# The last output group of a conformer layer in three token spans (256, 128, 128) instead of two halves

## The chip, the cores and the metric

One core of a Trainium2 chip runs the whole program. The metric is the device time of one execution in microseconds (us). The engines are named as in the profile: PE (TensorE matmuls), PEld (TensorE weight loads, which overlap PE), DVE (VectorE), ACT (ScalarE), POOL (GpSimd) and SP (SyncE, which issues the DMAs).

## What is computed

The reference at DEPTH = 1, with 512 tokens and a model width of 2048, is one conformer convolution module, one squared-ReLU MLP and a final norm, all in float32:

```python
h = x + conformer_conv(rms_norm(x, norm_mix_g), ...)
h = h + square(relu(rms_norm(h, norm_ffn_g) @ w_up)) @ w_down     # w_down: 8192 x 2048
return rms_norm(h, final_norm_g)       # y * rsqrt(mean(y*y, -1) + 1e-5) * g
```

## The kernel before

Activations lie transposed: 128 partitions hold 128 of the 2048 channels, and the free dimension holds the 512 tokens. The residual stream is `hT[0..3]`, four tiles of 4 x 512 columns. Each product of float32 operands is split in two float32r parts, and `mm3` makes it of three matmuls (hi x hi, hi x lo, lo x hi, L209 to L211), each with its own load of 128 x 128 weights.

The MLP's 8192 hidden channels come in units of 256. Every few units, a "down" job multiplies them by `w_down` and adds the result to `hT`. Its four output groups (512 output channels each) go through `group`: four PSUM banks, one for each 128 output channels `m`; pieces `p` of 256 rows of weights; and for each piece two blocks of rows `kk`, four `m` and three matmuls, so 24 matmuls for a piece. The last down job has four units, thus four pieces in a group (p = 0 to 3), 96 matmuls.

The last group of the last job is split by tokens. With `split` = 4 all four pieces run for the tokens 0 to 255 and then all four for 256 to 511, so 96 matmuls of 256 columns for each half; the loop over `m` is then outside that over `kk`. PE's order is the program's order. `hooks` are called ahead of the matmuls of a given (first token, piece, m) and put other work there. For the halves they are:

- (256, p 0, m 0): `finish(0)`: for each m, DVE adds the bank to `hT[3]` (L995), ACT squares it (L996), DVE adds the square to Q3 (L998, L1000); then ACT multiplies by the norm's gain (L1003).
- (256, 0, 3): `fin_sum`: column sums of Q3 over the partitions, as plain float32 matmuls of one moving column with Q3 as the weights (L243); then DVE (`ms_fin`, L255), POOL (the power -1/2, L257) and DVE (`dg_fin`, L222) make a diagonal of the norm's scales.
- (256, 1, 2): `fin_scale`: one plain float32 matmul (L232) spreads the scales to all partitions. Nine multiplications (`fin_parts`: two of one 128-channel row of blocks, seven of two) scale `hT`; two of them are on POOL. Nine stores on SP's queue follow (L1034).
- (256, 3, 0): `fin_head`: the column sums of Q3 for the second half, which holds only groups 0 to 2; the squares of group 3 are added at the end, with four more parts.

After the last matmul of the group stand `finish(256)`, `fin_sum(256)` and `fin_scale(256)`, with all nine multiplications on DVE. In blocks under `manual_schedule(engines=ordered)` the work of DVE, ACT and POOL stays in the order written.

Of the kernel before, what the change touches and what calls it, by code (L numbers as in the profile page):

```python
# [8 lines left out]
F32 = mybir.dt.float32  # L9
# [5 lines left out]
P = 128  # L15
T = 512
# [11 lines left out]
HT = T // 2  # L28
# [18 lines left out]
LN_FIRST = (3, 6)  # L47
UNIT = 256
N_UNITS = DFF // UNIT
FIN_POOL = (4, 8), ()  # L50


@with_exitstack
def conformer_layer(ctx: ExitStack, tc: tile.TileContext, xT, vecs, wdw, w1, w2, wupb, wdn, outT):
    nc = tc.nc
# [3 lines left out]
    wpool = ctx.enter_context(tc.tile_pool(name="wpool", bufs=WBUFS))  # L59
# [26 lines left out]
    def col(base, k):  # L86
        return vec[:, base + k : base + k + 1]
# [109 lines left out]
    def prep(upto):  # L197
        fetch(upto + 2)
        while state["prep"] < min(upto, len(pieces)):
            i = state["prep"]  # L200
            state["prep"] += 1
            if pieces[i][1] is BLOCKS:
                split_blocks(i)
                continue
            split_hi(i)
            split_lo(i, nc.gpsimd if FIRST_POOL <= i < n_p1 else nc.vector)
# [8 lines left out]
    def bank(tag, name):  # L215
        return pp.tile([P, T], F32, tag=tag, name=name, bufs=banks_of[tag])

    def diag(r, name, pool):
        n = r.shape[1]
        tag, bufs = ("diag", 2) if pool is ph1 else ("z", 3)  # L220
        dg = pool.tile([P, 4, P], F32, tag=tag, name=f"dg_{name}", bufs=bufs)[:, 0:n]
        nc.vector.tensor_tensor(  # L222
            out=dg,
            in0=ident[:, None, :].to_broadcast([P, n, P]),
            in1=r[:, :, None].to_broadcast([P, n, P]),
            op=ALU.mult,
        )
        return dg

    def spread(dg, out, start=True):  # L230

        nc.tensor.matmul(  # L232
            out, lhsT=ones, rhs=dg.rearrange("p a b -> p (a b)"), start=start, stop=True, skip_group_check=True
        )
        return out

    def colsum(b, c0, parts, t0, n, first, last, neg=0):

        for i, part in enumerate(parts):
            for t in range(n):
                nc.tensor.matmul(  # L243
                    b[:, c0 + t : c0 + t + 1],
                    lhsT=part[:, t0 + t * P : t0 + (t + 1) * P],
                    rhs=invd[:, neg : neg + 1],
                    start=first and i == 0 and t == 0,
                    stop=last and i == len(parts) - 1,
                    skip_group_check=True,
                )  # L250

    def rms_scale(b, name, pool, n=4):

        ms = pool.tile([P, n], F32, tag=f"ms{n}", name=f"ms_{name}", bufs=2)
        nc.vector.tensor_scalar_add(out=ms, in0=b[:, 0:n], scalar1=EPS)  # L255
        r = pool.tile([P, n], F32, tag=f"rr{n}", name=f"rr_{name}", bufs=2)
        nc.gpsimd.tensor_tensor(out=r, in0=ms, in1=mhalf[:, 0:n], op=ALU.pow)  # L257
        return diag(r, name, pool)


    p1 = ExitStack()
# [63 lines left out]
    ordered = {mybir.EngineType.DVE, mybir.EngineType.Activation, mybir.EngineType.Pool}  # L325
    with tc.manual_schedule(engines=ordered):
        for k in range(NK):
            ah[k], al[k] = split_scaled(k, x_of(k), col(C_GMIX, k))
            i, kk = divmod(k, 2)
            if i < 2 or kk == 0:  # L330
# [4 lines left out]
                    out=lo[:, :, part], in0=r, in1=hi[:, :, part].bitcast(F32), op=ALU.subtract  # L335
# [44 lines left out]
    box = {}  # L380
# [376 lines left out]
    ng = {"n": 0}  # L757
    pi = {"i": n_p1}

    def group(nk, rows_hi, rows_lo, hooks=None, split=0):  # L760


        n = ng["n"]
        ng["n"] += 1
        banks = box["banks"] = [bank("mm" if n % 2 == 0 else "xxxy"[m], f"g{n}_{m}") for m in range(4)]
        i0 = pi["i"]
        pi["i"] += nk // 2
        spans = [(h * HT, HT, p) for h in range(2) for p in range(split)]
        spans += [(0, T, p) for p in range(split, nk // 2)]
        for t0, w, p in spans:  # L770
            prep(i0 + p + 3 if t0 or w == T else min(i0 + p + 3, i0 + split))
            wh, wl = prepped[i0 + p]
            tok = slice(t0, t0 + w)
            order = [(kk, m) for kk in range(2) for m in range(4)]
            if w < T:
                order = [(kk, m) for m in range(4) for kk in range(2)]
            for kk, m in order:
                if hooks and kk == 0 and (t0, p, m) in hooks:
                    hooks[t0, p, m]()
                k = 2 * p + kk  # L780
                c = slice(m * P, (m + 1) * P)
                mm3(
                    banks[m][:, tok],
                    wh[:, kk, c],
                    wl[:, kk, c],
                    rows_hi[k][:, tok],
                    rows_lo[k][:, tok],
                    k == 0 and t0 == 0,
                    k == nk - 1,
                    skip_group_check=split > 0,  # L790
                )
        return banks
# [34 lines left out]
    for g in range(4):  # L827
        hooks = {}
        if g == 0:
            hooks = dict(zip(LN_AT, (second_taps, second_sums, second_scale)))  # L830
        if g == 3:

            hooks = {(0, 2 + 2 * i, 0): (lambda kt: lambda: place(kt, blocks_of[kt]))(3 + i) for i in range(3)}
        banks = group(NK, sh, sl, hooks, split=4 if g == 0 else 0)
        if g == 0:
            ph2 = ctx.enter_context(tc.tile_pool(name="ph2", bufs=2, reuse_waits="tile"))
# [5 lines left out]
        for m in range(4):  # L842
            k = 4 * g + m
            h = hT[g][:, m, :]
            nc.vector.scalar_tensor_tensor(
                out=h, in0=banks[m], scalar=col(C_BPW2, k), in1=h, op0=ALU.add, op1=ALU.add
            )
            if m % 2 == 0:
# [3 lines left out]
                out=blocks[:, at : at + 2].rearrange("p a b -> p (a b)"), in_=h, func=AF.Copy, scale=col(C_GFFN, k)  # L852
# [100 lines left out]
    Q3 = None  # L953
    for kind, what in jobs[:-1]:
# [4 lines left out]
        for g in range(4):  # L959
            banks = group(2 * len(what), zh, zl)  # L960
            for m in range(4):
                h = hT[g][:, m, :]
# [4 lines left out]
    Q3 = ph2.tile([P, T], F32, tag="Q2", name="Q3", bufs=1)  # L967
    sqo = [ph2.tile([P, 7, T], F32, tag=f"T{i}", name=f"sqo{i}", bufs=1) for i in range(3)]

    def sq_of(k):  # L970
        return sqo[k // 7][:, k % 7, :]

    for g in range(3):
        banks = group(kc, zh, zl)
        for m in range(4):
            k = 4 * g + m
            h = hT[g][:, m, :]
# [8 lines left out]


    sqs = [sq_of(12 + m) for m in range(4)]

    def finish(t0):  # L990
        tok = slice(t0, t0 + HT)
        with tc.manual_schedule(engines=ordered):
            for m in range(4):
                h = hT[3][:, m, tok]
                nc.vector.tensor_add(out=h, in0=h, in1=box["banks"][m][:, tok])  # L995
                nc.scalar.activation(out=sqs[m][:, tok], in_=h, func=AF.Square)  # L996
                if t0 == 0 and m:
                    nc.vector.tensor_add(out=Q3[:, tok], in0=Q3[:, tok], in1=sqs[m - 1][:, tok])  # L998
            if t0 == 0:
                nc.vector.tensor_add(out=Q3[:, tok], in0=Q3[:, tok], in1=sqs[3][:, tok])  # L1000
            for m in range(4):
                h = hT[3][:, m, tok]
                nc.scalar.activation(out=h, in_=h, func=AF.Copy, scale=col(C_GFIN, 12 + m))  # L1003

    def fin_sum(t0=0):
        if t0 == 0:
            b = bank("mm", "cs_fin0")
            colsum(b, 0, [Q3], t0, 2, True, True)
        else:
            b = box["csb"]  # L1010
            colsum(b, 0, sqs, t0, 2, False, True)
        with tc.manual_schedule(engines=ordered):
            box["dg"] = rms_scale(b, f"fin{t0}", ph2, 2)

    def fin_head():
        box["csb"] = bank("mm", "cs_finb")
        colsum(box["csb"], 0, [Q3], HT, 2, True, False)

    def fin_scale(t0=0):
        tok = slice(t0, t0 + HT)  # L1020
        rf = spread(box["dg"], bank("mm", f"sp_fin{t0}")[:, 0:HT])
        rfs = ph2.tile([P, T], F32, tag="W", name=f"rfs{t0}", bufs=1)[:, 0:HT]
        with tc.manual_schedule(engines=ordered):
            if FIN_POOL[t0 > 0]:
                nc.scalar.copy(out=rfs, in_=rf)
            for i, (g, m, n) in enumerate(fin_parts):
                h2 = hT[g][:, m : m + n, tok]
                if i in FIN_POOL[t0 > 0]:
                    nc.gpsimd.tensor_mul(out=h2, in0=h2, in1=rfs[:, None, :].to_broadcast([P, n, HT]))
                else:  # L1030
                    nc.vector.tensor_mul(out=h2, in0=h2, in1=rf[:, None, :].to_broadcast([P, n, HT]))
        for g, m, n in fin_parts:
            k = 4 * g + m
            nc.sync.dma_start(  # L1034
                out=outT[k * P : (k + n) * P, tok].rearrange("(k p) t -> p k t", p=P),
                in_=hT[g][:, m : m + n, tok],
            )

    fin_parts = [(0, 0, 1), (0, 1, 1)] + [(i // 2, i % 2 * 2, 2) for i in range(1, 8)]

    group(
        kc,
        zh,
        zl,
        {(HT, 0, 0): lambda: finish(0), (HT, 0, 3): fin_sum, (HT, 1, 2): fin_scale, (HT, 3, 0): fin_head},
        split=kc // 2,
    )
    finish(HT)
    fin_sum(HT)
    fin_scale(HT)  # L1050


# [48 lines left out]
```

## Time and profile before

| | us |
|---|---|
| median of 3 runs | 1927.95 (1926.95 to 1928.57) |
| profiled execution, its own time | 1929.58 |
| its span, first to last instruction | 1927.5 |
| PE busy | 1905.0 (99% of the span) |
| DVE / ACT / POOL busy | 1377.4 / 742.4 / 349.4 |
| first matmul of the last group | 1889.90 from the span's start |
| first matmul of its second half | 1901.41 |
| last matmul of the group | 1914.11 |

PE is busy nearly throughout. Only the last 13 us, after the last matmul of the group, belong to the other engines and the stores. A timeline row gives the start, the length, the engine, the line and the operation with its output and input; matmuls overlap in time, so that the distance between two starts, not the length, is what one costs in a stream.

### The profile page before, as it was taken

Reading aid. Unit: us, or ns where it says so; the run is one execution under the profiler, and the core shown is the slowest. Engines: PE = TensorE matmul, PEld = TensorE weight load, DVE = VectorE, ACT = ScalarE, POOL = GpSimd, SP = SyncE. Lnnn points to the kernel's source line nnn. Section 1 sums busy time; section 2 is a strip of 40 time slices with the busy share of each in tenths; the row PEclk is TensorE's granted clock in tenths of the full one; section 3 lists DMA queues with packets and bytes.
Section 4 is the critical chain, followed back from the end, with each engine's and each line's share of the span. In section 5 each row is a group of like instructions: output and inputs, shape, how many; then the busy total and the mean of one; then the engine's idle time right before and its main releaser. Section 6 shows DMA issues by size and latency. Waiting matters only on the chain.

```text
span 1927.5 us, 27676 instructions
## 1 busy us (share of the span) xinstructions
PE 1905.0 (99%) x11200; PEld 1699.8 (88%) x11200; DVE 1377.4 (71%) x1910; ACT 742.4 (39%) x910; POOL 349.4 (18%) x240
## 2 busy tenths in 40 slices
PE   9999999999999999999999999999999999999997
PEld 8888888888889898998989899898989989898987
DVE  6899998975568676776667677676767767676845
ACT  6544444554344242323324232332423324242433
POOL 1788998741211000000000000000000000000000
PEclk9999999999999999999999999999999999999999
DMA  7333333142323333323233332333333233233332
GB/s 247 88 99 98 99 89 109 46 147 93 98 83 104 99 110 89 117 90 111 88 99 116 93 110 88 110 94 102 112 88 110 88 120 92 96 110 91 118 98 99
DMA packets 134559, 199.24 MB, mean 103 GB/s; under 512 B 7200, under 2 KB 72992, under 8 KB 134432
## 3 DMA queue, kind: packets, MB, share of 16 engines
q1 hardware_dynamic: 134288, 197.41, 33.5%
q8 instruction: 87, 1.43, 0.3%
q14 instruction: 40, 0.33, 0.1%
q10 hardware_dynamic: 144, 0.07, 0.0%
HBM read 193.27 MB, written 4.19 MB: 102 GB/s over the span
## 4 chain that ended last, share of the span: by engine, by line
issue 68%; PE 26%; DVE 3%; POOL 1%; ACT 1%; DMA 0%; POOLq 0%; SPq 0%; DVEq 0%; ACTq 0%
PE g L210 3%; PE g L209 3%; PE g L211 3%; PE pa L210 2%; PE pg L211 2%; PE pg L210 2%; PE pa L211 2%; PE pg L209 2%; PE pa L209 2%; DVE acc L434 1%; PE pa L372 1%; PE pg L372 1%; DMA wr<-w 0%; POOL Q L859 0%; PE u L211 0%
## 5 line engine op out<-in xcount | busy, mean ns | idle before, releaser
L171 ACT CAST wh<-wr 128x1024 fp32r<-128x1024 f32 x215 | 225.7, 1050 | 500.1 <-PE g L210 321.1
L209 PE MATMUL g<-z,wh 128*128 128x512 f32 (+1 forms) x1016 | 391.1, 385 | 0.0
L210 PE MATMUL g<-z,wh 128*128 128x512 f32 (+1 forms) x1016 | 390.8, 385 | 0.0
L211 PE MATMUL g<-z,wl 128*128 128x512 f32 (+1 forms) x1016 | 390.7, 385 | 0.0
L176 DVE TENSOR_TENSOR wl<-wr,wh 128x1024 fp32r<-128x1024 f32 x158 | 201.1, 1273 | 207.8 <-ACT wh L171 207.7
L211 PE MATMUL u<-slot,wl 128*128 128x256 f32 x1120 | 317.8, 284 | 1.6 <-DVE wl L195 1.0
L209 PE MATMUL u<-slot,wh 128*128 128x256 f32 x1120 | 318.0, 284 | 0.0
L210 PE MATMUL u<-slot,wh 128*128 128x256 f32 x1120 | 317.5, 283 | 0.0
L195 DVE TENSOR_TENSOR wl<-ws,wh 128x1024 fp32r<-128x1024 f32 x128 | 156.7, 1224 | 160.2 <-ACT wh L194 160.2
L434 DVE SCALAR_TENSOR_TENSOR acc<-u,wd,acc 128x512 f32<-128x512 f32 (+1 forms) x360 | 238.6, 735 | 4.6 <-ACT acc L430 3.9
L257 POOL TENSOR_TENSOR rr_fin<-ms_fin,mhalf 128x2 f32<-128x2 f32 x2 | 1.4, 695 | 1309.6 <-DVE ms_fin L255 1309.6
L211 PEld LDWEIGHTS g<-z,wl 128*128 128x128 f32 x1016 | 191.0, 188 | 37.7
L209 PEld LDWEIGHTS g<-z,wh 128*128 128x128 f32 x1016 | 191.1, 188 | 37.3
L210 PEld LDWEIGHTS g<-z,wh 128*128 128x128 f32 x1016 | 191.1, 188 | 37.1
L211 PEld LDWEIGHTS u<-slot,wl 128*128 128x128 f32 x1120 | 215.4, 192 | 2.0 <-DVE wl L195 1.2
L209 PEld LDWEIGHTS u<-slot,wh 128*128 128x128 f32 x1120 | 215.4, 192 | 0.2 <-issue 0.2
L210 PEld LDWEIGHTS u<-slot,wh 128*128 128x128 f32 x1120 | 215.3, 192 | 0.2 <-issue 0.2
L187 ACT CAST wh<-wr 128x768 fp32r<-128x768 f32 x128 | 106.9, 835 | 275.5 <-PE u L210 152.5
L194 ACT CAST wh<-ws 128x1024 fp32r<-128x1024 f32 x128 | 133.9, 1046 | 178.5 <-PE g L210 69.7
L211 PE MATMUL u<-T,wl 128*128 128x256 f32 x672 | 190.6, 284 | 0.9 <-DVE wl L193 0.9
L210 PE MATMUL u<-T,wh 128*128 128x256 f32 x672 | 190.5, 284 | 0.0
L209 PE MATMUL u<-T,wh 128*128 128x256 f32 x672 | 190.4, 283 | 0.0
(214 smaller groups left out, 3432.2 us busy)
## 6 DMA issues: line engine op xcount, KB each, us to landing
wr<-wupb SPq DMA_DIRECT2D x128, 512.0 KB, 3.6
wr<-wdn SPq DMA_DIRECT2D x128, 512.0 KB, 3.7
wr<-w SPq DMA_DIRECT2D x128, 256.0 KB, 3.3
wr<-w SPq DMA_DIRECT2D x32, 512.0 KB, 3.7
h<-xT SPq DMA_DIRECT2D x4, 1024.0 KB, 11.8
outT<-h SPq DMA_DIRECT2D x14, 256.0 KB, 2.9
x<-xT SPq DMA_DIRECT2D x6, 512.0 KB, 8.1
x<-xT SPq DMA_DIRECT2D x4, 256.0 KB, 4.8
```

The lines of the kernel that those rows point to most:

```text
L171: nc.scalar.copy(out=prepped[i][0], in_=r)
L176: eng.tensor_tensor(out=lo, in0=r, in1=hi.bitcast(F32), op=ALU.subtract)
L187: nc.scalar.copy(out=hr, in_=r[:, :, 1:4])
L194: nc.scalar.copy(out=hs, in_=s)
L195: nc.vector.tensor_tensor(out=ls, in0=s, in1=hs.bitcast(F32), op=ALU.subtract)
L209: nc.tensor.matmul(out, lhsT=wh, rhs=xh, start=start, stop=False, **kw)
L210: nc.tensor.matmul(out, lhsT=wh, rhs=xl, start=False, stop=False, **kw)
L211: nc.tensor.matmul(out, lhsT=wl, rhs=xh, start=False, stop=stop, **kw)
L257: nc.gpsimd.tensor_tensor(out=r, in0=ms, in1=mhalf[:, 0:n], op=ALU.pow)
L372: nc.tensor.matmul(banks[j][s], lhsT=w[:, s, k % 2, c], rhs=x, start=k == 0 and x is ah[k] and w is wh, stop=stop)
L434: nc.vector.scalar_tensor_tensor(out=acc if c < end - 1 else vt, in0=u[:, c : c + n], scalar=wd[:, j, c : c + 1], in1=src, op0=ALU.mult, o ...
```

## The change

The last group runs in three spans of tokens: 0 to 255, 256 to 383, 384 to 511. `group` gets the list `cuts`, and for each cut it runs its four pieces again: 96 matmuls of 256 columns and twice 96 of 128. Each span has its own norm and stores. The work of `fin_scale` is divided in `fin_spread` (the matmul, and for span 0 a copy for POOL) and `fin_scale(i, some)` over `early` (parts 0 to 4) and `late` (parts 5 to 8) with their stores.

```diff
-        spans = [(h * HT, HT, p) for h in range(2) for p in range(split)]
+        cuts = cuts or ((0, HT), (HT, HT))
+        spans = [(t0, w, p) for t0, w in cuts for p in range(split)]
...
+        if pool is wpool:
+            tag, bufs = "ws", 2
...
+    cuts = (0, HT), (HT, P), (HT + P, P)
...
+            b = box["csb"][:, i - 1 : i]
+            colsum(b, 0, sqs, t0, 1, False, True)
         with tc.manual_schedule(engines=ordered):
-            box["dg"] = rms_scale(b, f"fin{t0}", ph2, 2)
+            box["dg"] = rms_scale(b, f"fin{i}", ph2, n // P, wpool)
...
+    early, late = range(FIN_CUT), range(FIN_CUT, len(fin_parts))
+    def first_scale():
+        fin_spread(0)
+        fin_scale(0, early)
+    def second_finish():
+        finish(1)
+        fin_scale(0, late)
+    def second_scale_up():
+        fin_spread(1)
+        fin_scale(1, early)
+    t1, t2 = HT, HT + P
     group(kc, zh, zl,
-        {(HT, 0, 0): lambda: finish(0), (HT, 0, 3): fin_sum, (HT, 1, 2): fin_scale, (HT, 3, 0): fin_head},
+        {
+            (t1, 0, 0): lambda: finish(0),
+            (t1, 1, 1): lambda: fin_sum(0),
+            (t1, 2, 3): first_scale,
+            (t1, 3, 1): fin_head,
+            (t2, 0, 0): second_finish,
+            (t2, 1, 3): lambda: fin_sum(1),
+            (t2, 3, 2): second_scale_up,
+        },
         split=kc // 2,
+        cuts=cuts,
     )
-    finish(HT)
-    fin_sum(HT)
-    fin_scale(HT)
+    finish(2)
+    fin_scale(1, late)
+    fin_sum(2)
+    fin_spread(2)
+    fin_scale(2, range(len(fin_parts)))
```

The diagonals of the scales also move from the buffers "z" to the buffers "ws", whose last use lies in the split of the last up weights.

## Rows read from the trace of the kernel before

**Rows 1.** The page, busy time by engine: us, share, number of instructions.

```profile
PE 1905.0 (99%) x11200; PEld 1699.8 (88%) x11200; DVE 1377.4 (71%) x1910; ACT 742.4 (39%) x910; POOL 349.4 (18%) x240
```

**Rows 2.** Timeline of PE, second half: start us, us, engine, line, operation.

```profile
1901.41 0.28 PE L209 MATMUL g<-z,wh 128*128 128x256 f32 x1
...
1903.45 0.28 PE L211 MATMUL g<-z,wl 128*128 128x256 f32 x1
...
1914.11 0.28 PE L211 MATMUL g<-slot,slot 128*128 128x256 f32 x1
```

**Rows 3.** Timeline of DVE, the last add and what follows it.

```profile
1914.43 0.42 DVE L995 TENSOR_TENSOR h<-h,g 128x256 f32<-128x256 f32 x1 [0.29 <-PE g L211]
1916.11 0.16 DVE L255 TENSOR_SCALAR ms_fin<-cs_finb 128x2 f32<-128x2 f32 x1 [1.26 <-PE cs_finb L243]
1917.08 0.43 DVE L222 TENSOR_TENSOR dg_fin<-ident,rr_fin 128x256 f32<-128x256 f32 x1 [0.81 <-POOL rr_fin L257]
1918.30 4.94 DVE L1031 TENSOR_TENSOR h<-h,sp_fin 128x256 f32<-128x256 f32 x9 [0.79 <-PE sp_fin L232]
```

**Rows 4.** Timeline of SP, the last nine stores.

```profile
1918.74 5.22 SPq L1034 DMA_DIRECT2D outT<-h  x9
```

**Rows 5.** Timeline of PE in the stretch of 512 columns ahead of the last group.

```profile
1885.14 0.39 PE L209 MATMUL g<-slot,wh 128*128 128x512 f32 x1
...
1889.45 0.39 PE L210 MATMUL g<-slot,wh 128*128 128x512 f32 x1
```

**Rows 6.** One-column matmuls: their loads, their lengths (ns min/median/max), and eight in a stream.

```profile
1914.11 1.88 PEld L243 LDWEIGHTS cs_finb<-invd,sqo 128*128 128x128 f32 x16
...
L243 PEld LDWEIGHTS cs_finb<-invd,sqo x16: 192/192/193, 1914.1 to 1915.8; 128*128 128x128 f32 x16
L243 PE MATMUL cs_finb<-invd,sqo x16: 168/251/251, 1914.2 to 1915.8; 128*128 128x1 f32 x16
...
598.43 0.95 PE L243 MATMUL u<-invd,Q 128*128 128x1 f32 x8
599.24 0.36 PE L209 MATMUL u<-slot,wh 128*128 128x256 f32 x1
599.44 0.28 PE L210 MATMUL u<-slot,wh 128*128 128x256 f32 x1
```

**Rows 7.** Weight loads: plain float32 at the start (mean ns), then float32r (timeline).

```profile
L266 PEld LDWEIGHTS warm<-ones 128*128 128x128 f32 x16 | 3.5, 330 | 1.0 <-DVE ones L66 1.0
...
8.80 0.33 PEld L372 LDWEIGHTS pa<-slot,wh 128*128 128x128 f32 x1
...
11.52 0.19 PEld L372 LDWEIGHTS pa<-slot,wl 128*128 128x128 f32 x1
```

**Rows 8.** Groups by line and form, multiplications and the squares: busy us, mean ns.

```profile
L1031 DVE TENSOR_TENSOR h<-h,sp_fin 128x512 f32<-128x512 f32 x12 | 7.3, 680 | 0.0
L1031 DVE TENSOR_TENSOR h<-h,sp_fin 128x256 f32<-128x256 f32 x4 | 1.5, 418 | 2.5 <-ACT rfs L1025 1.7 <-PE sp_fin L232 0.8
L996 ACT ACTIVATE sqo<-h 128x256 f32<-128x256 f32 x8 | 3.3, 418 | 12.6 <-DVE h L995 12.6
```

**Rows 9.** All stores: issue ns min/median/max; DMA issues by size, us to landing.

```profile
L1034 SPq DMA_DIRECT2D outT<-h x18: 344/411/678, 1907.7 to 1923.3; - x18
...
outT<-h SPq DMA_DIRECT2D x7, 256.0 KB, 2.7
outT<-h SPq DMA_DIRECT2D x2, 128.0 KB, 1.8
```

**Rows 10.** DMA queues from 100 to 300 us, weights in runs of 512 bytes: packets, MB, share.

```profile
q1 hardware_dynamic: 38876, 19.31, 33.3%
```

**Rows 11.** Groups of PE by form, 512 columns: float32r, then plain float32 (busy us, mean ns).

```profile
L209 PE MATMUL g<-z,wh 128*128 128x512 f32 x968 | 377.3, 390 | 0.0
...
L232 PE MATMUL sp_ffn<-dg_ffn,ones 128*128 128x512 f32 x2 | 1.0, 592 | 0.0
```

More of the change, by code (lines that the diff above doesn't have):

```diff
@@ L49 @@
 N_UNITS = DFF // UNIT
-FIN_POOL = (4, 8), ()
+FIN_POOL, FIN_CUT = (4, 8), 5
 @with_exitstack
@@ L250, in colsum, with rms_scale @@
                 )
-    def rms_scale(b, name, pool, n=4):
+    def rms_scale(b, name, pool, n=4, dpool=None):
         ms = pool.tile([P, n], F32, tag=f"ms{n}", name=f"ms_{name}", bufs=2)
@@ L257, in rms_scale @@
         nc.gpsimd.tensor_tensor(out=r, in0=ms, in1=mhalf[:, 0:n], op=ALU.pow)
-        return diag(r, name, pool)
+        return diag(r, name, dpool or pool)
     p1 = ExitStack()
@@ L758, in conformer_layer, with group @@
     pi = {"i": n_p1}
-    def group(nk, rows_hi, rows_lo, hooks=None, split=0):
+    def group(nk, rows_hi, rows_lo, hooks=None, split=0, cuts=None):
         n = ng["n"]
         ng["n"] += 1
+        cuts = cuts or ((0, HT), (HT, HT))
         banks = box["banks"] = [bank("mm" if n % 2 == 0 else "xxxy"[m], f"g{n}_{m}") for m in range(4)]
@@ L988, in conformer_layer, with finish @@
     sqs = [sq_of(12 + m) for m in range(4)]
-    def finish(t0):
-        tok = slice(t0, t0 + HT)
+    cuts = (0, HT), (HT, P), (HT + P, P)
+    def finish(i):
+        t0, n = cuts[i]
+        tok = slice(t0, t0 + n)
         with tc.manual_schedule(engines=ordered):
@@ L996, in finish @@
                 nc.scalar.activation(out=sqs[m][:, tok], in_=h, func=AF.Square)
-                if t0 == 0 and m:
+                if i == 0 and m:
                     nc.vector.tensor_add(out=Q3[:, tok], in0=Q3[:, tok], in1=sqs[m - 1][:, tok])
-            if t0 == 0:
+            if i == 0:
                 nc.vector.tensor_add(out=Q3[:, tok], in0=Q3[:, tok], in1=sqs[3][:, tok])
@@ L1003, in finish, with fin_head, fin_sum @@
                 nc.scalar.activation(out=h, in_=h, func=AF.Copy, scale=col(C_GFIN, 12 + m))
-    def fin_sum(t0=0):
-        if t0 == 0:
+    def fin_head():
+        box["csb"] = bank("mm", "cs_finb")
+        colsum(box["csb"], 0, [Q3], HT, 2, True, False)
+    def fin_sum(i):
+        t0, n = cuts[i]
+        if i == 0:
             b = bank("mm", "cs_fin0")
@@ L1009, in fin_sum, with fin_spread, fin_scale @@
         else:
-            b = box["csb"]
-            colsum(b, 0, sqs, t0, 2, False, True)
+            b = box["csb"][:, i - 1 : i]
+            colsum(b, 0, sqs, t0, 1, False, True)
         with tc.manual_schedule(engines=ordered):
-            box["dg"] = rms_scale(b, f"fin{t0}", ph2, 2)
[L1015 to L1022, printed above, removed]
+            box["dg"] = rms_scale(b, f"fin{i}", ph2, n // P, wpool)
+    def fin_spread(i):
+        n = cuts[i][1]
+        box["rf"] = spread(box["dg"], bank("mm", f"sp_fin{i}")[:, 0:n])
+        if i == 0:
+            box["rfs"] = ph2.tile([P, T], F32, tag="W", name="rfs", bufs=1)[:, 0:n]
+            with tc.manual_schedule(engines=ordered):
+                nc.scalar.copy(out=box["rfs"], in_=box["rf"])
+    def fin_scale(i, some):
+        t0, w = cuts[i]
+        tok = slice(t0, t0 + w)
         with tc.manual_schedule(engines=ordered):
-            if FIN_POOL[t0 > 0]:
-                nc.scalar.copy(out=rfs, in_=rf)
-            for i, (g, m, n) in enumerate(fin_parts):
+            for j in some:
+                g, m, n = fin_parts[j]
                 h2 = hT[g][:, m : m + n, tok]
-                if i in FIN_POOL[t0 > 0]:
-                    nc.gpsimd.tensor_mul(out=h2, in0=h2, in1=rfs[:, None, :].to_broadcast([P, n, HT]))
-                else:
-                    nc.vector.tensor_mul(out=h2, in0=h2, in1=rf[:, None, :].to_broadcast([P, n, HT]))
-        for g, m, n in fin_parts:
+                if i == 0 and j in FIN_POOL:
+                    nc.gpsimd.tensor_mul(out=h2, in0=h2, in1=box["rfs"][:, None, :].to_broadcast([P, n, w]))
+                else:
+                    nc.vector.tensor_mul(out=h2, in0=h2, in1=box["rf"][:, None, :].to_broadcast([P, n, w]))
+        for j in some:
+            g, m, n = fin_parts[j]
             k = 4 * g + m
```

## The prediction

> **What bounds the kernel now.** I read the page first: PE is busy for 99% of the span [rows 1], so time is only to be had where PE is, or in the tail behind its last matmul. Then the timeline of PE over the second half of the last group [rows 2]: its 96 matmuls of 256 columns start at 1901.41, and the last starts at 1914.11 and ends at X = 1914.39. From there to the end of the span at 1927.5 are 13.1 us, which the chain of the second half's norm and the stores make up [rows 3, 4]. The change means to shorten this tail, since less is left to do after the last matmul. It pays with PE: the same columns are cut in narrower matmuls, so the second half takes 192 matmuls and 192 loads of weights instead of 96. Whether that costs anything depends on one number, the distance of two matmuls of 128 columns in a stream, for which the trace has no row.
>
> **What a matmul of 128 columns costs.** The first 18 matmuls of the second half run undisturbed from 1901.41 to 1903.45 [rows 2]: 17 distances, 0.120 us each. In the stretch of 512 columns, 20 matmuls from 1885.14 to 1889.45 give 19 distances of 0.227 [rows 5]. So 256 columns fewer save 0.107, and if only columns counted, 128 columns would cost 0.120 - 0.053 = 0.067 us. That is the lower end. But each matmul brings its own load. The one-column matmuls of the norm have nothing to stream, and still their 16 loads take 1.88 us [rows 6]: (1.88 - 0.19)/15 = 0.113 each. The lengths say why: the first matmul takes 168 ns, those behind it in the stream 251, so they wait for their weights. Eight of them in the middle of a stream push the next matmuls back by 599.44 - 598.43 - 0.12 = 0.89 us, 0.111 each [rows 6]. So a load is not faster than about 0.11 us, and 256 columns just cover it.
>
> Those loads are plain float32, the ones in question float32r. They look alike wherever both are seen: both take 0.19 us late in the kernel, and at the very start, where loads are slow, both take 0.33 [rows 6, 7]. A load that ran at twice the speed would show it in one of these. I therefore take 0.113 us for 128 columns; the ends within this view are 0.111 and 0.120 (a matmul of half the columns should not cost more than the whole one). All of it assumes that loads still run beside the previous matmul, as they must at 0.120 for 256 columns.
>
> The Trainium skill weighs in here on both sides. Its page "TensorE: Matmul & The Clock Gate", section "LDWEIGHTS (loading the stationary operand)", puts a load at its columns divided by 1.2 per ns, so an estimate of 107 ns for 128; by that rule, which the row of 0.113 us bears out, the change is a loss. The same page in "Back-to-back issue gap" gives N/2.4 + 2.5 ns, an estimate of 56 ns, for a matmul without its load, by which the narrow matmuls would be free; that is the first rival below.
>
> **PE's side of the sum.** Before, from the first to the last start of the second half is 12.70 us; 95 distances of 0.120 are 11.40, so 1.30 went to what the hooks insert (two column sums of four instructions, one spread). After: 191 x 0.113 = 21.58; the 1.30 again; the column sum of span 1, eight one-column instructions, 0.89 as measured [rows 6]; and a spread of 128 columns, between 0.2 and 0.4 since a spread of 256 has about 1.3 - 2 x 0.45 = 0.4, taken as 0.3. Sum 24.07 us. The last matmul comes 24.07 - 12.70 = 11.4 us later; with 0.111 or 0.120, 11.0 to 12.7.
>
> **The tail.** Let X' be the new end of the last matmul. DVE's multiplications take 0.68 us for 512 columns and 0.42 for 256 [rows 8], with about 0.08 of overlap between neighbours (7 x 0.60 + 2 x 0.34 + 0.08 = 4.96, against 4.94 in [rows 3]); on the same line 128 columns take 0.29, that is 0.21 in a row. ACT's square, 0.42 for 256 [rows 8], becomes about 0.3.
>
> - The spread of span 1 stands 12 matmuls ahead of the end and is ready at about X' - 1.3. Then come, in DVE's fixed order, the five early multiplications of span 1 (2 x 0.21 + 3 x 0.34 = 1.4, to X' + 0.1), the four adds of span 2 (to X' + 1.0), and four late multiplications (1.4, to X' + 2.3). Only then comes `ms_fin`; the last square and column sum are ready earlier, at X' + 1.8. Before, `ms_fin` started at 1916.11 = X + 1.7 [rows 3]. So the norm of the last span starts some 0.6 us later than it did: this is the added wait, and POOL, the diagonal and the last nine multiplications stand behind it.
> - From `ms_fin` to the first multiplication it took 2.19 us [rows 3]. The diagonal and the spread are half as wide: 1.9. First product at X' + 4.2, done at X' + 4.5, the ninth at 4.2 + 2 x 0.21 + 7 x 0.34 + 0.1 = X' + 7.1 (before, X + 8.85).
> - Nine stores follow on SP. Before, they went at DVE's pace, 5.22 us [rows 4]; now SP may set it, with 0.41 us for one [rows 9]: 3.7, to X' + 8.2. From the end of the last issue (1918.74 + 5.22) to the end of the span were 3.54 us; a store of 128 KB lands 0.9 sooner than one of 256 KB [rows 9], which leaves 2.65. End at X' + 10.9, against X + 13.1: 2.2 us saved. With SP at 0.344 or 0.678 for each, it is 2.8 saved or 0.2 lost.
> - Packets become 512 bytes long. Weights in such runs took 200 x 0.333 x 16/38876 = 27.4 ns each [rows 10], so the last 2048 packets on 16 engines need 3.5 us, within SP's 3.7. That was read from HBM; that a write is alike is assumed.
>
> What else moves costs nothing while the third span lasts (some 11 us of PE): the adds of span 1 and three late multiplications of 256 tokens, 2.7 us of DVE, are done before its column sum is due (42 matmuls, 4.7 us); POOL's late part and its extra power, the earlier stores, and the extra instructions of ACT lie there too. If matmuls were fast, these 42 would last 2.8 us, and PE could wait 0 to 0.3. The buffers "ws" for the diagonals have long been free.
>
> Sum: + 11.4 - 2.2 = + 9.2 us, from + 8.2 (11.0 - 2.8) to + 12.9 (12.7 + 0.2). The profiled execution took 1929.58 for a span of 1927.5 and would take 1938.8; it lies 1.63 above the median of 1927.95. On the median: 1937.1, from 1936.1 to 1940.9.
>
> **Rivals.**
>
> - *Only columns count (not slower).* Loads of float32r are faster than the plain ones, or hide fully. Distance 0.067: 191 x 0.067 + 2.49 - 12.70 = + 2.6 on PE; the tail saves about 1.5, since DVE's queue stands later against X'. Time + 1.1: 1929.1, from 1927.7 to 1931. For it speaks that 256 and 512 columns differ by columns alone; against it the 0.113 and the equal lengths of loads. It decides below a distance of 0.085, where the sum falls under 3.9 us. Even here nothing pays back the two extra norms on PE, so a clear gain is hardly to be had.
> - *Loads partly hidden (a smaller loss).* A distance halfway between 0.067 and 0.113, 0.09: 191 x 0.09 + 2.49 - 12.70 = + 7.0, less 1.9: 1933.0. No row speaks for a value between; it stands for an overlap that the one-column rows can't show. The same section of that page also reports 81 ns for a stream of such pairs, an estimate of 1931.6 here; its 131 ns for 512 columns stands against 227 in this trace [rows 5].
> - *Narrow matmuls lose the float32r rate (much slower).* If the narrow ones run as plain float32 does, each would go through the array twice at half the rate. Plain float32 takes 592 ns where float32r takes 390 [rows 11], 0.20 more per pass for 512 columns, so one pass streams 0.41, 0.10 for 128 columns; two passes with their loads come to 0.23. Then 191 x 0.23 + 2.49 - 12.70 = + 33.7, less 2: 1960. No row has float32r under 256 columns, so nothing excludes it.
>
> **How the numbers follow.** Load-bound matmuls 0.74, columns alone 0.15, partly hidden 0.03, the lost rate 0.08. The likeliest gives 1937.1. The range takes in its bounds and the two cases beneath it, from 1928.5 to 1941, and leaves out the lost rate and the outer edges. By 0.2% (3.9 us, about what a measurement of this kernel can tell from no change): slower 0.74 + 0.08 + 0.03 = 0.85; columns alone is split in same 0.13 and faster 0.02, for its lower edge and a tail shorter than worked out.
>
> **What would show it.** In the timeline of PE, matmuls of 128 columns should start 0.113 us apart, loads with no gap between them, and the last one at about 1925.5. The tail behind it should be 10.9 us, with `ms_fin` right behind late multiplications of span 1, and the nine last stores bound by SP. A distance near 0.07 would make the prediction wrong downwards, one near 0.2, or two instructions for one product, upwards.

## The result and the profile after

The changed kernel takes 1948.45 us (median of 4, 1946.95 to 1951.92) against 1928.26 for the kernel before on the same chip: ratio 1.0104, 95% interval 1.0091 to 1.0117, 20.2 us slower. The forecast was slower, 1937.1, with a range up to 1941.0: the sign was right, and the loss is twice what was worked out.

From the first matmul of the second half to the end of the span it is 1945.02 - 1898.78 = 46.2 us in the profile after and 1927.5 - 1901.41 = 26.1 before [rows 2]: 20.1 us, the whole difference. (The profiled execution of after reaches that point 2.6 us earlier, since its matmuls of 512 columns between 5.6 and 10 us are 0.23 us apart, those of before 0.43.) So everything lies in the second and third span and the tail. The page's first line, to set beside [rows 1]:

```profile
PE 1924.0 (99%) x11298; PEld 1718.7 (88%) x11298; DVE 1377.2 (71%) x1925; ACT 743.8 (38%) x918; POOL 350.6 (18%) x241
```

PE has 98 instructions more: 96 matmuls and a spread of two. No product was issued twice. The timeline of PE in spans 1 and 2 (start us, us, engine, line, operation; in brackets the idle time ahead and what ended it):

```profile
1898.78 0.22 PE L209 MATMUL g<-z,wh 128*128 128x128 f32 x1
1898.85 0.28 PE L210 MATMUL g<-z,wh 128*128 128x128 f32 x1
...
1901.97 0.27 PE L211 MATMUL g<-z,wl 128*128 128x128 f32 x1
...
1910.67 0.27 PE L211 MATMUL g<-slot,slot 128*128 128x128 f32 x1
1911.63 0.33 PE L209 MATMUL g<-z,wh 128*128 128x128 f32 x1 [0.69 <-DVE h L1000]
...
1912.69 0.38 PE L209 MATMUL g<-z,wh 128*128 128x128 f32 x1
1912.86 0.41 PE L210 MATMUL g<-z,wh 128*128 128x128 f32 x1
1913.07 0.41 PE L211 MATMUL g<-z,wl 128*128 128x128 f32 x1
...
1933.13 0.41 PE L211 MATMUL g<-slot,slot 128*128 128x128 f32 x1
```

Three things are to be read here. From 1898.85 to 1901.97 are 28 distances of 0.111 us: narrow matmuls (128 columns) cost what a load of weights costs [rows 6], as forecast. At the start of the third span PE waits 0.69 us for DVE. And from 1912.69, 1.06 us behind that wait, matmuls are 0.21 apart to the very end. The table by stage (length; busy us and count of PE, PEld, DVE, ACT and POOL; PEclk, the granted clock; share and GB/s of the DMA) names the reason:

```profile
1908.00:1911.00 3.00, 2.94 (x27) 2.80 (x26) 3.00 (x7) 0.00 (x0) 2.21 (x2) 1.00 0.61 200
1913.00:1923.00 10.00, 10.00 (x49) 10.00 (x49) 0.45 (x2) 0.69 (x3) 0.55 (x1) 0.50 0.25 82
1923.00:1933.00 10.00, 10.00 (x49) 10.00 (x48) 2.45 (x9) 0.62 (x2) 0.00 (x0) 0.50 0.04 12
```

TensorE's granted clock was at its upper level (1.00, 2.4 GHz) until then and at the lower one (0.50, 1.2 GHz) for the next 20 us, with PE busy all the time. The wait itself, in the timeline of DVE:

```profile
1907.64 3.74 DVE L1043 TENSOR_TENSOR h<-h,sp_fin 128x256 f32<-128x256 f32 x7 [3.57 <-ACT rfs L1031]
1911.30 0.87 DVE L1000 TENSOR_TENSOR h<-h,g 128x128 f32<-128x128 f32 x4
```

Seven multiplications of span 0 (four early ones, and the three late ones of DVE, which the scheduler put ahead of the adds, since their blocks may pass each other) keep DVE until 1911.3. The first add of span 1 takes 0.28 us and ends at 1911.57, and PE goes on at 1911.63: here the first matmul of a span into a bank waits for DVE's add from that bank, though the columns differ.

### The profile page after: what moved, and what is told of

It is laid out like the page before. It is cut to its first block, busy times and chain, and to the rows that moved or that the text cites. A ratio compares the mean times of both kernels' runs of the same rounds, so it can differ in the third digit from the quotient of the medians.

```text
span 1945.0 us, 27914 instructions
## 1 busy us (share of the span) xinstructions
PE 1924.0 (99%) x11298; PEld 1718.7 (88%) x11298; DVE 1377.2 (71%) x1925; ACT 743.8 (38%) x918; POOL 350.6 (18%) x241
## 4 chain that ended last, share of the span: by engine, by line
PE 95%; DVE 2%; issue 1%; POOL 1%; ACT 1%; DMA 0%; POOLq 0%; DVEq 0%; ACTq 0%
PE g L210 15%; PE g L209 15%; PE g L211 15%; PE u L211 11%; PE u L209 11%; PE u L210 11%; PE pa L211 3%; PE pa L210 3%; PE pa L209 3%; PE pg L211 3%; PE pg L210 3%; PE pg L209 3%; PE pa L374 1%; PE pg L374 1%; DVE acc L436 1%
## 5 line engine op out<-in xcount | busy, mean ns | idle before, releaser
L209 PE MATMUL g<-z,wh 128*128 128x512 f32 (+2 forms) x1040 | 399.8, 384 | 0.7 <-DVE h L1000 0.7
L210 PE MATMUL g<-z,wh 128*128 128x512 f32 (+2 forms) x1040 | 399.7, 384 | 0.0
L211 PE MATMUL g<-z,wl 128*128 128x512 f32 (+2 forms) x1040 | 399.5, 384 | 0.0
L209 PEld LDWEIGHTS g<-z,wh 128*128 128x128 f32 x1040 | 198.5, 191 | 38.2 <-DVE h L1000 0.8
L211 PEld LDWEIGHTS g<-z,wl 128*128 128x128 f32 x1040 | 198.5, 191 | 37.8
L210 PEld LDWEIGHTS g<-z,wh 128*128 128x128 f32 x1040 | 198.6, 191 | 37.2
```

What stands on the lines that cost most here:

```text
L209: nc.tensor.matmul(out, lhsT=wh, rhs=xh, start=start, stop=False, **kw)
L210: nc.tensor.matmul(out, lhsT=wh, rhs=xl, start=False, stop=False, **kw)
L211: nc.tensor.matmul(out, lhsT=wl, rhs=xh, start=False, stop=stop, **kw)
```

## The experiments

Two questions: is the rest of the forecast right once the clock stays up, and what let the clock fall, the narrow matmuls (theory A), the wait (B), or both together (C, formed from e1 to e3)? Wide matmuls are those of 256 columns or more. Where one execution is named, there was no other.

### e1: the wait taken away

```diff
     def second_finish():
-        finish(1)
-        fin_scale(0, late)
+        with tc.manual_schedule(engines=ordered):
+            finish(1)
+            fin_scale(0, late)
```

> The changed kernel with the adds of span 1 ahead of the late multiplications of span 0 on DVE, so that PE need not wait at the start of the third span (it waited 0.69 us there). Theory A (narrow matmuls alone let TensorE's clock fall to its lower level): the clock still falls within a few us of where it fell, 13.9 us after the first narrow matmul, and the time stays near 1948 (1944 to 1952). Theory B (the wait of PE lets it fall): the clock stays at the upper level to the last matmul, matmuls of 128 columns stay 0.112 us apart, and the time is 1937 (1935 to 1939), as predicted before.

Measured: 1938.82 us (median of 4) against 1928.73, ratio 1.0062 (1.0037 to 1.0086). The adds now stand behind four multiplications instead of seven, PE crosses into the third span without a pause, and the clock stays up. Timeline of PE, then the stage table of e1:

```profile
1911.66 0.27 PE L211 MATMUL g<-slot,slot 128*128 128x128 f32 x1
1911.77 0.27 PE L209 MATMUL g<-z,wh 128*128 128x128 f32 x1
...
1923.49 0.28 PE L211 MATMUL g<-slot,slot 128*128 128x128 f32 x1
```

```profile
1900.00:1911.00 11.00, 11.00 (x99) 10.95 (x98) 4.08 (x12) 2.71 (x8) 3.02 (x3) 1.00 0.07 25
1912.00:1923.00 11.00, 11.00 (x101) 11.00 (x101) 3.54 (x11) 2.10 (x7) 0.55 (x1) 1.00 0.40 137
```

Three of the four executions took 1937.3 to 1939.5; one took 1946.19 at a mean granted clock of 0.989 (the others 0.994 or 0.995), so there the clock was low for longer, though this wait had been taken away. That execution has no trace, and a mean doesn't tell where in the kernel the clock was low (e4 has an example).

### e2: the wait alone, among wide matmuls

```diff
         with tc.manual_schedule(engines=ordered):
+            if t0 == 0:
+                for i in range(2):
+                    s = wpool.tile([P, 4, HT], F32, tag="ws", name=f"idle{i}", bufs=2)
+                    nc.vector.tensor_copy(out=s, in_=box["banks"][0][:, None, tok].to_broadcast([P, 4, HT]))
             for m in range(4):
```

(In `finish` of the kernel before.)

> The kernel before, halves of 256 columns, with two copies on DVE (about 2.4 us, into a tile that nobody reads) ahead of its first add, so that PE waits some 0.8 us between the halves. Theory A (narrow matmuls): the clock stays up, the time is that of before plus about 0.8 us, 1929. Theory B (the wait): the clock falls soon behind the wait and the second half takes up to twice its 12.7 us, 1935 to 1940.

Measured: one execution, 1930.65. PE waited, and the clock stayed at its upper level behind the wait:

```profile
1901.51 0.38 PE L209 MATMUL g<-z,wh 128*128 128x256 f32 x1 [0.62 <-DVE h L999]
```

```profile
1902.00:1914.00 12.00, 11.60 (x96) 11.34 (x95) 7.03 (x17) 3.46 (x9) 3.25 (x3) 1.00 0.37 124
```

The trace of before says the same of three earlier waits among 256 columns, of 0.64, 0.99 and 0.86 us; the longest of them, and the stage with all three:

```profile
579.45 0.39 PE L211 MATMUL u<-slot,wl 128*128 128x256 f32 x1 [0.99 <-DVE wl L195]
```

```profile
575.00:590.00 15.00, 12.51 (x100) 11.90 (x99) 11.58 (x15) 5.85 (x8) 6.84 (x2) 1.00 0.33 93
```

### e3: narrow matmuls alone, for 21.4 us, inside the last job

```diff
-        spans = [(h * HT, HT, p) for h in range(2) for p in range(split)]
+        spans = [(t0, w, p) for t0, w in cuts for p in range(split)]
...
-            prep(i0 + p + 3 if t0 or w == T else min(i0 + p + 3, i0 + split))
+            prep(i0 + p + 3 if t0 == cuts[-1][0] or w == T else min(i0 + p + 3, i0 + split))
...
+    narrow = tuple((t * P, P) for t in range(4))
     for g in range(3):
-        banks = group(kc, zh, zl)
+        banks = group(kc, zh, zl, None, 2, narrow) if g == 1 else group(kc, zh, zl)
```

> The kernel before, with the second group of the last down job run in four spans of 128 columns for its first two pieces (192 narrow matmuls, 21.5 us at 0.112 instead of 10.9 us), and no norm, wait or store between them; 512 columns follow. Theory A (narrow matmuls): the clock falls within that stretch, about 14 us after its start, and rises again after the return to 512 columns; time 1928 + 10.7 + 6 to 12, that is 1944 to 1951. Theory B (the wait): no fall, 1939.

Measured: one execution, 1939.19, 10.5 above before, as the distances alone make it. The narrow stretch in the stage table:

```profile
1846.00:1866.00 20.00, 20.00 (x182) 20.00 (x180) 4.39 (x6) 5.04 (x8) 0.00 (x0) 1.00 0.09 28
```

So neither A nor B as put: 20 us of narrow matmuls without a pause kept the clock up, and a wait of 0.62 us among wide ones did too.

### e4: spans of 384 and 128 tokens

The kernel before with `cut = 3 * P` in place of the half: `cuts=((0, cut), (cut, P))`, and the hooks at (cut, 0, 0), (cut, 1, 0), (cut, 2, 0) and (cut, 3, 0).

> Two spans, of 384 and 128 tokens: only 96 narrow matmuls, some 11 us, at the very end. PE's side by the distances of the traces: 96 x 0.173 + 96 x 0.112 = 27.4 instead of 96 x 0.240 = 23.0 for both halves, + 4.4; the tail saves about 2 as in the changed kernel at the upper clock. Theory A (narrow matmuls, after a time): 11 us are less than the 13.9 after which the clock fell, so it stays up and the time is 1930 (1928 to 1932). If the clock falls earlier, 1933 to 1941. Theory B (the wait): no wait, 1930.

Measured: 1931.84 (median of 10) against 1928.73, ratio 1.0017 (1.0008 to 1.0027), slightly slower, within the forecast. PE did not wait at the seam, and the clock stayed up through the narrow span:

```profile
1910.47 0.22 PE L209 MATMUL g<-z,wh 128*128 128x128 f32 x1
```

```profile
1911.00:1922.00 11.00, 11.00 (x97) 10.74 (x96) 6.11 (x11) 3.03 (x6) 4.48 (x3) 1.00 0.21 79
```

A shorter last span costs more on PE than it brings in the tail here too. The execution with the trace was the slowest of the ten (1936.08, mean clock 0.991), and its clock fell elsewhere, among 256 columns behind a wait of 1.74 us, with another of 1.51 us before it rose:

```profile
578.28 0.39 PE L211 MATMUL u<-slot,wl 128*128 128x256 f32 x1 [1.74 <-DVE wl L193]
582.79 0.58 PE L211 MATMUL u<-slot,wl 128*128 128x256 f32 x1 [1.51 <-DVE wl L195]
```

```profile
580.00:586.00 6.00, 4.49 (x21) 4.19 (x21) 6.00 (x8) 1.04 (x1) 0.00 (x0) 0.50 0.38 114
```

So an execution can be some 4 us longer, at a lower mean clock, without a fall in the last group.

### e5: the wait put back into e1

```diff
         with tc.manual_schedule(engines=ordered):
+            for n in (8, 4):
+                s = wpool.tile([P, n, P], F32, tag="ws", name=f"idle{n}", bufs=2)
+                b = box["banks"][0][:, None, HT : HT + P]
+                nc.vector.tensor_copy(out=s, in_=b.to_broadcast([P, n, P]))
             finish(1)
```

> The kernel of e1, with two copies on DVE (1.7 us, into a tile that nobody reads) ahead of the adds of span 1: the order stays that of e1, only PE's wait of some 0.7 us at the start of the third span is back. Theory C (a wait among narrow matmuls lets the clock fall, neither alone does): the clock falls within some 3 us behind the wait and stays low to the last matmul; time 1945 to 1952. If the order of DVE's work, or chance, made e1 fast: 1939.5, e1 plus 0.7.

Measured: 1949.36 (median of 4, all between 1946.87 and 1949.52) against 1929.61, ratio 1.010 (1.0083 to 1.0117). That is the changed kernel's loss again, with another cause of the wait. All eight executions with the wait (the changed kernel and e5) took 1946.87 or more; of the nine without it (e1 and e9), eight took 1941.75 or less. Timeline of PE at the wait and the stage behind it:

```profile
1913.51 0.33 PE L209 MATMUL g<-z,wh 128*128 128x128 f32 x1 [0.62 <-DVE h L1000]
```

```profile
1914.00:1924.00 10.00, 10.00 (x50) 10.00 (x49) 1.97 (x5) 1.57 (x6) 0.00 (x0) 0.50 0.33 115
1924.00:1934.00 10.00, 10.00 (x49) 10.00 (x48) 1.43 (x7) 0.62 (x2) 0.55 (x1) 0.50 0.00 0
```

### e6: a longer wait among wide matmuls

As e2, with `range(4)` instead of `range(2)`.

> The kernel of e2 with four copies instead of two: halves of 256 columns, PE waits about 2.9 us between them. Theory C: with wide matmuls around it even this wait need not let the clock fall; 1928.7 + 3 = 1932, or, if a longer wait does it with wide matmuls too, 1935 to 1943 with a clock that comes back within the second half.

Measured: one execution, 1933.65. The clock did fall here, but it was back after some 3.4 us, within the half. Timeline of PE, and the stages behind the wait:

```profile
1903.40 0.58 PE L209 MATMUL g<-z,wh 128*128 128x256 f32 x1 [2.88 <-DVE h L999]
```

```profile
1904.00:1907.00 3.00, 3.00 (x16) 3.00 (x16) 2.01 (x6) 2.26 (x7) 0.00 (x0) 0.52 0.00 0
1908.00:1916.00 8.00, 8.00 (x68) 7.95 (x67) 4.30 (x9) 0.37 (x1) 3.20 (x3) 1.00 0.46 154
```

### e7: a wait in the middle of e3's narrow stretch

```diff
+    def idle():
+        for n in (8, 8, 4):
+            s = wpool.tile([P, n, P], F32, tag="ws", name=f"idle{n}", bufs=2)
+            b = box["banks"][0][:, None, P : 2 * P]
+            nc.vector.tensor_copy(out=s, in_=b.to_broadcast([P, n, P]))
...
-        banks = group(kc, zh, zl, None, 2, narrow) if g == 1 else group(kc, zh, zl)
+        banks = group(kc, zh, zl, {(2 * P, 0, 0): idle}, 2, narrow) if g == 1 else group(kc, zh, zl)
```

> The kernel of e3 (192 narrow matmuls inside the last job), with copies on DVE by which PE waits 0.5 to 1 us at their middle; 10.8 us of narrow matmuls follow, then 512 columns. Theory C: the clock falls behind the wait, the rest of the narrow stretch takes up to twice its time, and the clock rises again among the 512 columns; 1939 + 1 + 6 to 12, that is 1946 to 1952. If narrow matmuls and a wait do not suffice: 1940.

Measured: one execution, 1952.19, 13 more than e3. Timeline of PE at the wait and where 512 columns come back, then the stages:

```profile
1859.08 0.33 PE L209 MATMUL g<-z,wh 128*128 128x128 f32 x1 [1.04 <-DVE idle L979]
...
1878.23 0.41 PE L211 MATMUL g<-z,wl 128*128 128x128 f32 x1
1878.44 0.73 PE L209 MATMUL g<-z,wh 128*128 128x512 f32 x1
...
1881.01 0.40 PE L209 MATMUL g<-z,wh 128*128 128x512 f32 x1
```

```profile
1861.00:1870.00 9.00, 9.00 (x44) 9.00 (x43) 0.00 (x0) 0.00 (x0) 0.00 (x0) 0.50 0.01 2
1882.00:1890.00 8.00, 8.00 (x37) 6.64 (x36) 2.53 (x3) 1.63 (x2) 0.00 (x0) 1.00 0.32 111
```

The clock fell behind the wait, stayed down for all narrow matmuls that were left, and was up again 2.6 us after the first matmul of 512 columns.

### e8: wide ahead of the wait, narrow behind it

The kernel of e4 with three copies of 1024 columns from bank 0, as in e5, ahead of the adds of `finish(0)`.

> The kernel of e4 (384 and 128 tokens) with copies on DVE by which PE waits about 1 us between the spans: wide matmuls ahead of the wait, narrow ones only behind it. Theory C in its strict form (narrow on both sides): no fall, 1932 + 1 = 1933. If narrow matmuls behind the wait suffice: the clock falls within some 5 us, and the time is 1938 to 1943.

Measured: one execution, 1941.93, the time of the second case. But three shorter pauses follow the wait before the clock is down: two starts, at 1908.46 and 1909.39, come 0.2 us late, and PE waits 0.27 us ahead of a column sum at 1910.54. These have narrow matmuls ahead of them and behind them, so the run doesn't exclude the strict form of C; which of the four pauses it was, it can't say.

```profile
1906.85 0.33 PE L209 MATMUL g<-z,wh 128*128 128x128 f32 x1 [0.92 <-DVE h L1003]
...
1908.13 0.28 PE L211 MATMUL g<-z,wl 128*128 128x128 f32 x1
1908.46 0.33 PE L209 MATMUL g<-z,wh 128*128 128x128 f32 x1
...
1910.54 1.44 PE L243 MATMUL cs_fin<-invd,Q 128*128 128x1 f32 x6 [0.27 <-DVE Q L1008]
```

```profile
1907.00:1910.00 3.00, 2.90 (x23) 2.61 (x24) 2.75 (x7) 1.97 (x5) 0.00 (x0) 1.00 0.00 0
1914.00:1924.00 10.00, 10.00 (x45) 9.39 (x45) 4.86 (x7) 0.48 (x1) 3.61 (x2) 0.50 0.31 114
```

### e9: the tail in the order that the prediction assumed

```diff
-    finish(2)
-    fin_scale(1, late)
+    with tc.manual_schedule(engines=ordered):
+        finish(2)
+        fin_scale(1, late)
     fin_sum(2)
```

(On e1.)

> The kernel of e1 with the adds of the last span ahead of the late multiplications of span 1 on DVE, the order that the prediction had assumed for the tail (in e1 all nine multiplications stand ahead of the last two adds). By the prediction's steps the last norm starts 0.5 us earlier against the last matmul, at X' + 2.3 instead of X' + 2.8, and the tail shrinks from 12.3 us to 11.5 to 12. Time 1938 where the clock stays up, still some 9 us slower than before. Should the clock fall in some of its executions without a wait of PE, as it seems to have done in one of four of e1, those take 1944 to 1952.

Measured: 1938.26 (median of 5) against 1928.86, ratio 1.0053 (1.0039 to 1.0067). The last matmul starts at 1924.38 and ends at X' = 1924.66. Timeline of DVE in e1, and then in e9:

```profile
1922.51 2.80 DVE L1043 TENSOR_TENSOR h<-h,sp_fin 128x128 f32<-128x128 f32 x9
1925.23 0.48 DVE L1000 TENSOR_TENSOR h<-h,g 128x128 f32<-128x128 f32 x2
1926.55 0.16 DVE L257 TENSOR_SCALAR ms_fin<-cs_finb 128x1 f32<-128x1 f32 x1 [0.84 <-PE cs_finb L245]
```

```profile
1923.41 1.48 DVE L1043 TENSOR_TENSOR h<-h,sp_fin 128x128 f32<-128x128 f32 x5
1924.80 0.48 DVE L1000 TENSOR_TENSOR h<-h,g 128x128 f32<-128x128 f32 x2
1925.20 1.41 DVE L1043 TENSOR_TENSOR h<-h,sp_fin 128x256 f32<-128x256 f32 x4
1926.52 0.15 DVE L257 TENSOR_SCALAR ms_fin<-cs_finb 128x1 f32<-128x1 f32 x1
1928.41 2.81 DVE L1043 TENSOR_TENSOR h<-h,sp_fin 128x128 f32<-128x128 f32 x9 [0.78 <-PE sp_fin L234]
```

In e1 (X' = 1923.77) all nine multiplications of span 1 stand ahead of the last two adds, and `ms_fin` comes at X' + 2.8; in e9 it comes at X' + 1.9. The tail is 12.3 us in e1 and 11.1 in e9 (1935.8 - 1924.66). One of the five executions took 1941.75 at a mean clock of 0.991. It has no trace either; in time lost and mean clock it is like e4's traced execution, whose clock fell far from the last group.

## Why the prediction was right in sign and wrong in size

- **Distance of narrow matmuls: right.** 0.111 us, at the lower edge of the 0.111 to 0.120 that was given. The rivals "only columns count" (0.067), "partly hidden" (0.09) and "the lost rate" (0.23) are out, as long as the clock is up. The 0.213 behind the wait is close to the lost rate's price, but it comes with the clock at 0.50, and in e1 the same matmuls are 0.111 apart. The Trainium skill's rule for loads ("TensorE: Matmul & The Clock Gate", "LDWEIGHTS (loading the stationary operand)"; an estimate of 107 ns) agrees with the 111 ns. Its N/2.4 + 2.5 ("Back-to-back issue gap", an estimate of 56 ns) is given for a matmul without its load, and these streams, in which each matmul brings its own weights, don't show it.
- **PE's sum: right where the clock stays up.** In e1 the stretch from the first narrow start (1899.77) to the last is 23.7 us, against 24.07 worked out and 12.70 before.
- **The tail: right mechanism, order mistaken.** 2.2 us of saving were worked out. With the assumed order, e9 saves 13.1 - 11.1 = 2.0. That this is so near is partly luck: the first product came at X' + 3.75 instead of X' + 4.2, and the nine stores took SP 4.5 us instead of 3.7 (0.51 from one to the next instead of 0.41). The scheduler's own order lets DVE's multiplications pass the adds and leaves a saving of 0.8 (e1).
- **The sum without the fall: right.** + 9.2 worked out, + 9.4 in e9, + 10.1 in e1.
- **The step that failed** is "What else moves costs nothing while the third span lasts", in two ways. It asked of DVE's work between the spans only whether it was done before the next column sum, not who waits for the adds: PE did, 0.69 us, at its first matmul of the third span. And it took DVE's adds and late multiplications in the order written, where their blocks can pass each other. In the halves of before the add of bank 0 ended 1.5 us ahead of the first matmul of the second half (1901.41 [rows 2]); here seven multiplications stood in front of it.
- **And the price of that wait was not its length.** The wait was 0.69 us, but behind it the clock was at 0.50. From 1912.69 to 1933.13 there are 86 more starts, 0.102 us slower each: 8.8 us, and about 0.9 for the column sum and the spread among them, which take twice as long too. The wait itself puts 0.96 us between two starts instead of 0.11, so 0.85 more, and the first matmuls behind it and the last one are 0.2 longer. That is 10.8; the tail took 11.5 instead of e1's 12.3, since more of DVE's work was done before the slow stream ended. Together 10.0 from the first narrow matmul to the end, by the two traces; the medians on the chip are 9.6 apart (1948.45 - 1938.82). The prediction doesn't mention the clock, and no rival had it: each narrow matmul was priced at the upper level. The trace of before has it at 1.00 throughout the last group, but not everywhere. At a wait of 2.72 us in the middle of the kernel it went to 0.50 for some 7 us.

The rows of the kernel before that the last two points rest on: the add of bank 0 (DVE), then that wait (PE) and its stage.

```profile
1899.46 0.42 DVE L995 TENSOR_TENSOR h<-h,g 128x256 f32<-128x256 f32 x1 [4.92 <-PE g L211]
```

```profile
407.41 0.58 PE L210 MATMUL g<-slot,wh 128*128 128x256 f32 x1 [2.72 <-DVE slot L613]
```

```profile
406.70:413.40 6.70, 5.99 (x24) 5.70 (x25) 6.70 (x6) 3.55 (x6) 4.59 (x3) 0.50 0.20 73
```

What let it fall, as far as the runs show: a wait of 0.6 to 1.0 us with narrow matmuls on both sides of it, in every trace that has one (after, e5, e7), and in e8, where wide ones stood ahead of the wait but shorter pauses followed among narrow ones. Narrow matmuls without a pause did not (e1, e3, e4, e9), nor did waits of 0.6 to 1.0 us among 256 columns (e2, and before as shown there). Longer waits among 256 columns did in some traces (2.72 us in before, 2.88 in e6, 1.74 in e4) and not in another: the wait of e4 lasts 1.73 us in e7, another of 2.10 us follows, and the clock is 1.00 from 575 to 590 us. So the length alone doesn't decide. What makes the fall expensive is the way back: among dense matmuls of 256 or 512 columns the clock rose again within some 4 us (e6, e7), while among narrow matmuls it stayed down for 18 to 21 us with PE busy, as long as they lasted (after, e5, e7, e8).

The Trainium skill, page "TensorE: Matmul & The Clock Gate", section "HAM oscillation — how this bites in real kernels", tells of a kernel with few output rows that loses the clock in waits of 3 to 5 us for DMAs. No run here repeats that case; in these runs waits of 0.62 to 1.04 us for DVE were enough where narrow matmuls stood around them.

What stays open: why the clock falls at one wait and not at another of the same length, how short a wait still does it, and what happened in the two single executions of e1 and e9 that were slower without the known wait.

None of the versions with narrow spans beats the kernel before; e4, the nearest, is 0.17% slower.

## What to carry to other kernels

Before a stream of matmuls is cut narrower, find rows in which weight loads have nothing to hide behind: if a load takes nearly as long as the wide matmul (0.11 against 0.12 us here), the narrow ones cost nearly the same each and there are more of them. Ask of every engine that reads an accumulator bank whom it keeps waiting at the next matmul into that bank, and what else stands in its queue before the read. And in a stretch of narrow matmuls count a short wait of TensorE not by its length alone: in the traces with such a wait, nearly all matmuls behind it, up to the next wide ones, ran at half the clock.

## What the hardware showed that was not expected

- At the upper clock, narrow streams (0.111 us per matmul of 128 columns) ran for 20 us at a granted clock of 1.00 (e3); once down, the same stream, now 0.21 us apart, ran for 20 us at 0.50 with PE busy throughout (the changed kernel). Both levels lasted with the same kind of matmul.
- One wait of 0.6 to 0.7 us thus cost about 10 us (e5 is 19.8 us above its kernel before, e1 10.1).
- The first matmul of the third span waited for DVE's read of other columns of the same bank and started 0.06 us after the end of that add (the changed kernel).
